# Two transformer blocks on one core: small first loads with matmuls on a constant ahead of them, side banks for a third product, and the last product one token half after the other

## The chip, the cores and the metric

The kernel runs on one NeuronCore of a Trainium2 chip. A core has a matrix engine (TensorE, "PE" in the profile, with its weight loads as "PEld"), a vector engine (VectorE, "DVE"), a scalar engine (ScalarE, "ACT"), GpSimd ("POOL") and SyncE ("SP"), which here issues nearly all DMAs. Each engine works through its own instructions in order; semaphores tie them together. TensorE writes to PSUM, which has eight banks. The metric is the device time of one execution in microseconds; shown are three runs and one more execution taken with the hardware profiler.

## The reference

Input is `x`, 512 tokens of width 1024, in fp32. What is computed:

```
u  = rmsnorm(x) * norm_g
x += mixer1(u)          # 4 mLSTM heads of 256, and compressed/selected/windowed attention
x += ffn1(rmsnorm(x))   # gated: 2 x 2816 wide in, 2816 wide out, behind two norms folded into one factor
x += mixer2(rmsnorm(x)) # gated delta rule beside pooling
x += ffn2(rmsnorm(x))   # as ffn1
out = rmsnorm(x) * final_g
```

Each of the stages is modulated by vectors that an `ada` part computes from a conditioning input. The rmsnorm needs the sum of squares over all 1024 columns of a token before its factor (`rstd`) is known.

## The kernel before

The tokens lie along the free dimension: `x` is eight tiles of 128 channels x 512 tokens. A product is a `Group`: an output tile of 128 channels (or 256 to 512 columns "token-major") summed over `kts` tiles of 128 inputs, in an fp32 emulation of three matmuls, hi x hi, hi x lo and lo x hi, where hi is the value rounded to the matmul's fp32r and lo the rest. A group's weights come in pieces of at most 1024 columns. For each piece SP issues a DMA to `wr` (three buffers; `load`, L302), ScalarE casts it to `wh` and VectorE, or in the mixer every third time GpSimd, subtracts to get `wl` (`part`, L306). `run` (L323) walks over the plan, stays two pieces ahead with the splits and further ahead with the DMAs, and between the steps of a product calls `side_step`, which lets generators (the norm, gates, attention, mLSTM, `ada`) emit a little work of their own. A tile scheduler then fixes each engine's order. Products write to four PSUM banks of the pool `pg`, side work to the four of `pb` (`bank`).

At a norm, TensorE doesn't wait for `rstd`: the first products of a stage take `u = x * g` without the factor (`halves=True`: the token halves 0 to 255 and 256 to 511 go to two banks, each weight being used for both), and their evacuation `unorm` multiplies by `rbc`, the factor broadcast over the partitions. Meanwhile the generator `norm` runs: `colsum` into `nsum` (a matmul with `ones` over `nacc`, the sum of squares), `rstd`, a broadcast by matmul (`rb`, with its cast `rbc`), and then the eight normed inputs, `ht` and their hi and lo parts `hh` and `hl`. For FFN1 (`i == 0`) there are two norms in a row and so a second factor, `rr`.

At the start `setup` issues the loads: `cols` (all column constants), then `x` tile by tile with the pieces of the first weight `w_v0` between them (3, 3 and 2 of its 288-column k-tiles), `cst` (identity, masks), `posi`. `block1`'s `begin` then makes `uh` and `ul` (hi and lo of `u`) in the same order, on ScalarE and VectorE, in an order kept by hand, and behind it adds squares to `nacc`. The first product is `w_v0`, the next, `pe`, is `w_v1`, whose two pieces are taken together (`early`). The mLSTM's gates are side work: `lir`, `lfr` rows, a scan `mrow` on VectorE, and small products `gcol`, the last of them on `mrow`.

At the end, product 7 of FFN2's output (`ev_last`, L1466) runs with `halves`, both token halves alternating but for its last piece, which does half 0 and then half 1. Behind half 0's last matmul its residual `xr` and squares `sq7` are taken; `final_norm` (L1475) sums them on TensorE and takes the root on GpSimd; `final` (L1486) broadcasts the factor (`r1b`), multiplies (`fin`, 16 instructions of 128x256) and stores, in eight DMAs of 256 KB.

Of the kernel before, what the change touches and what calls it, by code (L numbers as in the profile page):

```python
# [9 lines left out]
F32 = mybir.dt.float32  # L10
# [8 lines left out]
P = 128  # L19
# [10 lines left out]
SOLVE_STEP = 4  # L30
SOLVE_DELAY = 7
NV = 2
NG = 3
# [124 lines left out]
class Group:  # L158


    def __init__(self, src, width, kts, xs, evac, token_major=False, pre=None, halves=False, mid=None, early=0):
        self.mid, self.early = mid, early
# [14 lines left out]
class Builder:  # L177
# [145 lines left out]
    def run(self, plan, ahead_dma=3, ahead_split=2):  # L323
# [5 lines left out]
        for g in plan:  # L329
# [6 lines left out]
            for k0, n in g.pieces:  # L336
# [41 lines left out]
                elif g.halves:  # L378
                    if k0 == 0:
                        ps = [self.pg.tile([P, 512], F32, tag="g", name="pg") for _ in range(2)]  # L380
                    if g.mid and k0 + n == g.kts:

                        for c, (e, f) in enumerate(((0, 256), (256, 512))):
                            for k in range(n):
                                xh, xl = g.xs()[k0 + k]
                                a, b = hi[:, k * wd:(k + 1) * wd], lo[:, k * wd:(k + 1) * wd]
                                self.mm(ps[c][:, :256], a, xh[:, e:f], False, False)
                                self.mm(ps[c][:, :256], a, xl[:, e:f], False, False)
                                self.mm(ps[c][:, :256], b, xh[:, e:f], False, k == n - 1)
                                if c and k == n // 2:  # L390
                                    g.mid()
                            g.evac(c, ps[c])
                        i += 1
                        continue
                    for k in range(n):
                        xh, xl = g.xs()[k0 + k]
                        kk = k0 + k
                        for w, x, first, last in ((hi, xh, kk == 0, False), (hi, xl, False, False),
                                                  (lo, xh, False, kk == g.kts - 1)):
                            for c, (e, f) in enumerate(((0, 256), (256, 512 if g.mid else 514))):  # L400
# [26 lines left out]
    def setup(self):  # L427
        nc = self.nc
        self.cst = self.const(max(e for _, e in self.coff.values()), "cst")
        self.cols = self.const(max(e for _, e in COLS.values()), "cols")  # L430
        self.posi = self.const(NT, "posi", I32)
        self.x = []
        nc.sync.dma_start(self.cols, self.A["cols"])
        for kt in range(KT):
            if kt % 3 == 0:
                self.load(kt // 3 + 1)
            s = self.slot("x")
            nc.sync.dma_start(s, self.A["xt"][:, kt])
# [5 lines left out]
        self.ones = self.const(P, "ones")  # L444
        nc.vector.memset(self.ones, 1.0)
        self.mhalf = self.const(32, "mhalf")
        nc.vector.memset(self.mhalf, -0.5)
# [67 lines left out]
    def norm(self, i):  # L515
# [12 lines left out]
        if i == 0:  # L528
# [6 lines left out]
            r1, r = r, rr  # L535
        self.rcol = r
        if i is None:
# [213 lines left out]
    def block1(self):  # L751
# [135 lines left out]
        for h in range(4):  # L887
            if h == 0:
                plan.append(self.start_norm(None))
                us = lambda: self.u  # L890
                G(W["w_v0"][0], 288, KT, us, ev_v(0), True)
                for i in range(1, NV):
# [496 lines left out]
    def ffn(self, j, i):  # L1389
# [47 lines left out]
        for f in range(NH):  # L1437
            for up in range(2):
                w = W[f"f{j}i"][f + up * NH]
                if f < 3:  # L1440
                    plan.append(Group(w, P, KT, lambda: self.u, ev_u(f, up), halves=True))
                else:
# [14 lines left out]
        for f in range(KT):  # L1457
            if i == 2 and f == KT - 1:
                plan.append(Group(W[f"f{j}o"][f], P, NH, lambda: self.act_, self.ev_last, halves=True,
                                  mid=lambda: self.final_norm(0)))  # L1460
            else:
# [4 lines left out]
    def ev_last(self, c, ps):  # L1466
# [6 lines left out]
        self.act(self.sq7[:, h], s[:, h], AF.Square)  # L1473

    def final_norm(self, c):  # L1475

        b = self.bank("n4")
        for t in range(2):
            s = slice((2 * c + t) * P, (2 * c + t + 1) * P)
            self.mm(b[:, t:t + 1], self.nacc[:, s], self.ones[:, 0:1], True, False)  # L1480
            self.mm(b[:, t:t + 1], self.sq7[:, s], self.ones[:, 0:1], False, True)
        v, self.nr[c] = self.small(2, "nv"), self.small(2, "nr")
        self.ts(v, b[:, 0:2], 1.0 / D, EPS, OP.mult, OP.add)
        self.pow(self.nr[c], v, 2)

    def final(self):  # L1486
        def bcast(c):
            b = self.bank("r1b")
            for t in range(2):
                self.mm(b[:, t * P:(t + 1) * P], self.nr[c][:, t:t + 1].to_broadcast([P, P]), self.ident)  # L1490
            return b

        b = bcast(0)
        self.final_norm(1)
        for c in range(2):
            for f in range(0, KT, 2):
                s = self.slot("fin").rearrange("p (f t) -> p f t", f=2)
                for e in range(2):
                    self.stt(s[:, e], self.x[f + e][:, c * 256:c * 256 + 256], self.c("final_g2", f + e, f + e + 1),
                             b[:, 0:256], OP.mult, OP.mult)  # L1500
                (self.nc.sync if f % 4 else self.nc.scalar).dma_start(
                    self.out[:, f:f + 2, c * 256:c * 256 + 256], s)
            if c == 0:
                b = bcast(1)

    def mixer(self):
# [485 lines left out]
```

## Time and profile before

| | us |
|---|---|
| three runs | 1960.74, 1965.48, 1965.86 |
| median | 1965.48 |
| profiled execution | 1959.12 |
| its span (first to last instruction) | 1957.3 |
| TensorE busy | 1909.8 |
| VectorE, ScalarE, GpSimd busy | 1157.4, 782.4, 293.5 |

The mean granted clock of TensorE over the span is 0.992 of full speed. A timeline's row gives the start, the duration of what it holds (one instruction, or several of the same kind in a row), and in brackets how long the engine stood idle before it and which instruction's end released it. Matmuls are pipelined: the duration of one is longer than the distance to the next, so pitches are taken between starts.

### The profile page before, as it was taken

To read this page: it belongs to the slowest core of one execution; us is meant where nothing else is said; L and a number is where in the kernel's file an instruction comes from. 1 tells how busy PE (TensorE), PEld (TensorE's weight loads), DVE (VectorE), ACT (ScalarE), POOL (GpSimd) and SP (SyncE) were. 2 spreads that over 40 slices of the span, in tenths; PEclk is the share of its full clock that TensorE was granted. 3 is DMA by queue.
4 is the path that set the end of the run, shared out by engine and by line. 5 is a ranking of instruction groups with operands and counts; after the bars stand their busy time and mean duration, and the time that the engine had idled before them with its cause. 6 is when DMAs were issued, how large, how long until landed. Compare 5 with 4: busy or idle time off the path is not lost. (4 is left out here: it accounts for less than half of the span.)

```text
span 1957.3 us, 26994 instructions
## 1 busy us (share of the span) xinstructions
PE 1909.8 (98%) x10296; PEld 1579.1 (81%) x10296; DVE 1157.4 (59%) x2307; ACT 782.4 (40%) x1568; POOL 293.5 (15%) x232
## 2 busy tenths in 40 slices
PE   8999999999999999999999998999999999999998
PEld 7889988887677888878888887777778898888887
DVE  7876554446446797774335677969645574333322
ACT  6444443434444432223224555564443342222221
POOL 2000000003220540000004232234020160000000
PEclk9999999999999999999999999999899999999999
DMA  5632224221103348883333233331232323333332
GB/s 198 202 101 87 76 76 151 78 87 57 52 28 116 116 139 260 263 263 112 106 116 95 80 89 100 93 88 55 72 124 86 126 90 97 97 97 93 91 90 72
DMA packets 89746, 216.17 MB, mean 110 GB/s; under 512 B 23569, under 2 KB 34705, under 8 KB 89617
## 3 DMA queue, kind: packets, MB, share of 16 engines
q1 hardware_dynamic: 84864, 208.27, 34.6%
q10 hardware_dynamic: 4752, 6.18, 1.0%
q8 instruction: 81, 1.33, 0.3%
q14 instruction: 49, 0.39, 0.1%
HBM read 206.55 MB, written 7.34 MB: 109 GB/s over the span
## 5 line engine op out<-in xcount | busy, mean ns | idle before, releaser
L217 ACT ACTIVATE wh<-wr 128x1024 fp32r<-128x1024 f32 (+4 forms) x311 | 315.1, 1014 | 626.7 <-PE pg L229 314.9
L220 DVE TENSOR_TENSOR wl<-wr,wh 128x1024 fp32r<-128x1024 f32 (+4 forms) x289 | 341.1, 1180 | 352.5 <-ACT wh L217 349.9
L229 PE MATMUL pg<-hh,wh 128*128 128x512 f32 x1240 | 500.5, 404 | 1.3 <-DVE un L220 1.3
L229 PE MATMUL pg<-hl,wh 128*128 128x512 f32 x1240 | 492.1, 397 | 0.0
L229 PE MATMUL pg<-hh,wl 128*128 128x512 f32 x1240 | 491.8, 397 | 0.3 <-DVE wl L220 0.3
L229 PEld LDWEIGHTS pg<-hh,wl 128*128 128x128 f32 x1240 | 234.0, 189 | 55.6 <-DVE wl L220 1.1
L229 PEld LDWEIGHTS pg<-hh,wh 128*128 128x128 f32 x1240 | 234.5, 189 | 52.1 <-issue 1.9
L229 PEld LDWEIGHTS pg<-hl,wh 128*128 128x128 f32 x1240 | 234.5, 189 | 50.3 <-issue 0.7
L229 PE MATMUL pg<-wh,hh 128*128 128x256 f32 (+2 forms) x512 | 157.8, 309 | 0.5 <-ACT hh L217 0.4
L229 PE MATMUL pg<-wh,hl 128*128 128x256 f32 (+2 forms) x512 | 151.4, 298 | 1.0 <-DVE hl L220 0.9
L229 PE MATMUL pg<-wl,hh 128*128 128x256 f32 (+2 forms) x512 | 151.5, 296 | 0.0
L229 PE MATMUL pg<-fah,wl 128*128 128x512 f32 (+1 forms) x374 | 140.0, 381 | 0.0
L229 PE MATMUL pg<-fah,wh 128*128 128x512 f32 (+1 forms) x374 | 139.9, 381 | 0.0
L229 PE MATMUL pg<-fal,wh 128*128 128x512 f32 (+1 forms) x374 | 139.8, 381 | 0.0
L220 POOL TENSOR_TENSOR nacc<-nacc,sq 128x512 f32<-128x512 f32 x34 | 47.6, 1405 | 611.0 <-ACT sq L217 610.9
L226 DVE SCALAR_TENSOR_TENSOR adaw<-adaw,sc 128x512 f32<-128x512 f32 x144 | 94.2, 687 | 37.1 <-DMA adaw<-in_ada 36.8
L226 DVE SCALAR_TENSOR_TENSOR ca<-cx,cols,ca 128x511 f32<-128x511 f32 (+2 forms) x120 | 99.3, 827 | 25.8 <-ACT ca L217 23.9
L229 PEld LDWEIGHTS pg<-wh,hh 128*128 128x128 f32 x512 | 96.7, 189 | 8.2 <-issue 3.7
L229 PEld LDWEIGHTS pg<-wl,hh 128*128 128x128 f32 x512 | 96.6, 189 | 4.3 <-issue 1.0
L229 PEld LDWEIGHTS pg<-wh,hl 128*128 128x128 f32 x512 | 95.9, 188 | 5.1 <-DVE hl L220 2.1
L229 PEld LDWEIGHTS pg<-fah,wh 128*128 128x128 f32 x374 | 69.3, 188 | 14.6
L229 PEld LDWEIGHTS pg<-fal,wh 128*128 128x128 f32 x374 | 69.2, 188 | 14.7
(429 smaller groups left out, 3065.9 us busy)
## 6 DMA issues: line engine op xcount, KB each, us to landing
adaw<-in_ada SPq DMA_DIRECT2D x72, 512.0 KB
wr<-in_f1i SPq DMA_DIRECT2D x44, 512.0 KB
wr<-in_f2i SPq DMA_DIRECT2D x44, 512.0 KB
wr<-in_m_qkv SPq DMA_DIRECT2D x24, 512.0 KB
wr<-in_w_o SPq DMA_DIRECT2D x16, 512.0 KB
wr<-in_f1o SPq DMA_DIRECT2D x16, 512.0 KB
wr<-in_m_g SPq DMA_DIRECT2D x16, 512.0 KB
wr<-in_f2o SPq DMA_DIRECT2D x16, 512.0 KB
```

What stands on the lines that cost most here:

```text
L217: return self.nc.scalar.activation(out, in_, f, bias=bias, scale=scale, **k)
L220: return (eng or self.nc.vector).tensor_tensor(out, a, b, op)
L226: return self.nc.vector.scalar_tensor_tensor(out, a, s, b, op0=op0, op1=op1, **k)
L229: return self.nc.tensor.matmul(out, lhsT, rhs, start=start, stop=stop, **k)
```

## The change

1. The start. `w_v0` comes in four pieces of 1, 2, 3 and 2 k-tiles (`FIRST`). A small tile `ng` with the columns of `norm_g` is loaded first; `cols` follows behind `x`. Nine matmuls of 128x128 on the constant `ones` stand first on TensorE. One piece more in block 1's list moves the split-ahead by one piece.
2. The norms. For FFN1 the norm generator takes one more step before `rb`. The third product on unnormed input (FFN's `f == 1` gate, the mixer's third `m_g`) takes its banks from `pb` (`alt`); the norm gives its own banks up sooner.
3. The last product does token half 0 over all its 22 k-tiles, and then half 1. At steps of half 1 the hook `final_mid` puts in half 0's sums, its root, its `r1b`, its eight `fin` and its four stores, and the sums over `nacc` for half 1.

```diff
+FIRST = [0, 1, 3, 6]
+WARM = 9
...
-        self.pieces = [(k, min(n, kts - k)) for k in range(0, kts, n)]
+        self.pieces = split or [(k, min(n, kts - k)) for k in range(0, kts, n)]
...
                 elif g.halves:
                     if k0 == 0:
-                        ps = [self.pg.tile([P, 512], F32, tag="g", name="pg") for _ in range(2)]
-                    if g.mid and k0 + n == g.kts:
...
+                        pool, tag = (self.pb, "b") if g.alt else (self.pg, "g")
+                        ps = [pool.tile([P, 512], F32, tag=tag, name="pg") for _ in range(2)]
+                    if g.mid:
+
+                        if k0 == 0:
+                            whole = []
+                        whole += [(hi, lo, k) for k in range(n)]
+                        if k0 + n == g.kts:
+                            for c, (e, f) in enumerate(((0, 256), (256, 512))):
+                                for kk, (hi, lo, k) in enumerate(whole):
...
+                                    if c:
+                                        g.mid(kk)
+                                g.evac(c, ps[c])
+                            whole = None
...
-        nc.sync.dma_start(self.cols, self.A["cols"])
+        self.ones = self.const(P, "ones")
+        nc.vector.memset(self.ones, 1.0)
+
+        b = self.bank("warm")
+        for _ in range(WARM):
+            self.mm(b[:, 0:P], self.ones, self.ones)
+        b = None
+        self.ng = self.const(KT, "ng")
+        nc.sync.dma_start(self.ng, self.A["cols"][:, COLS["norm_g"][0]:COLS["norm_g"][1]])
         for kt in range(KT):
-            if kt % 3 == 0:
-                self.load(kt // 3 + 1)
             s = self.slot("x")
             nc.sync.dma_start(s, self.A["xt"][:, kt])
             self.x.append(s)
-        self.load(3)
+            if kt in FIRST:
+                self.load(FIRST.index(kt) + 1)
+        nc.sync.dma_start(self.cols, self.A["cols"])
+        self.load(4)
...
+        if i == 0:
+            yield
         bc = self.rows_to_bcast(r, "rb")
         self.rbc = self.slot("rbc")
         self.act(self.rbc, bc)
+        bc = None
...
                 for kt in range(KT):
-                    if kt % 3 == 0:
-                        self.part(kt // 3 + 1)
-                    self.u_add(kt, self.x[kt], self.c("norm_g", kt, kt + 1))
+                    if kt in FIRST:
+                        self.part(FIRST.index(kt) + 1)
+                    self.u_add(kt, self.x[kt], self.ng[:, kt:kt + 1])
...
+                    plan.append(Group(w, P, KT, lambda: self.u, ev_u(f, up), halves=True,
+                                      alt=f == 1 and not up))
...
+    def final_mid(self, kk):
+
+        if kk == 4:
+            self.final_sum(0)
+            self.final_norm(0)
+        elif kk == 9:
+            self.final_out(0)
+        elif kk == NH - 3:
+            self.final_sum(1)
...
     def final(self):
...
         self.final_norm(1)
...
+        self.final_out(1)
...
-            G(W["m_g"][f], P, KT, us, ev_gu(("p", f)), halves=True)
+            G(W["m_g"][f], P, KT, us, ev_gu(("p", f)), halves=True, alt=f == 2)
```

The scheduler's orders show more than the diff. First ScalarE at the start. `uh` are the hi parts of the eight `u`, `gtr` is the first reader of `cst`, `wh` of 128x1024 is the first piece of `w_v1`. Before, from the sixth `uh` on:

```order
L217 ACTIVATE uh_153<-x_109,cols_92 128x512
L217 ACTIVATE wh_157<-wr_111 128x576
L217 ACTIVATE uh_161<-x_113,cols_92 128x512
L217 ACTIVATE uh_165<-x_115,cols_92 128x512
L217 ACTIVATE gtr_176<-cst_91 128x128
L217 ACTIVATE nacc_179<-x_97 128x512
L217 ACTIVATE sq_181<-x_99 128x512
```

Of the change, from the sixth `uh` on:

```order
L220 ACTIVATE uh_171<-x_124,ng_106 128x512
L220 ACTIVATE wh_175<-wr_128 128x576
L220 ACTIVATE uh_179<-x_126,ng_106 128x512
L220 ACTIVATE wh_282<-wr_220 128x1024
L220 ACTIVATE uh_183<-x_130,ng_106 128x512
L220 ACTIVATE gtr_194<-cst_91 128x128
L220 ACTIVATE nacc_197<-x_108 128x512
L220 ACTIVATE sq_199<-x_112 128x512
```

The cast of `w_v1`'s first piece now stands ahead of the last `uh`; before it stood behind the squares, further down than shown. VectorE's subtraction of the same piece moves with it, to a place ahead of the last `ul`.

Second TensorE at the mLSTM's gates, where the last `gcol` reads `mrow`, a scan on VectorE. Before, it stands 30 matmuls behind the `gcol` on `ones`, within the third product on normed input:

```order
L229 MATMUL pg_730<-hl_525,wh_563 128x512
L229 MATMUL pg_730<-hh_524,wl_564 128x512
L229 MATMUL gcol_677<-cst_91,mrow_650 128x4 x4
L229 MATMUL pg_730<-hh_528,wh_563 128x512
L229 MATMUL pg_730<-hl_529,wh_563 128x512
```

Of the change, 11 matmuls behind it, still within the second product:

```order
L232 MATMUL pg_682<-hh_519,wl_413 128x512
L232 MATMUL pg_682<-hh_550,wh_412 128x512
L232 MATMUL pg_682<-hl_551,wh_412 128x512
L232 MATMUL gcol_695<-cst_91,mrow_668 128x4 x4
L232 MATMUL pg_682<-hh_550,wl_413 128x512
L232 MATMUL pg_748<-hh_312,wh_581 128x512
```

So 19 matmuls that came ahead of it now follow it, while `mrow` has the same number in VectorE's order in both.

Third TensorE in FFN1's norm, where `rb` broadcasts the second factor `rr`. Before:

```order
L229 MATMUL pg_6714<-uh_6574,wl_6586 128x258
L229 MATMUL rb_6739<-cst_91,rr_6705 128x128 x4
L229 MATMUL pg_6713<-uh_6620,wh_6585 128x256
L229 MATMUL pg_6714<-uh_6620,wh_6585 128x258
L229 MATMUL pg_6713<-ul_6621,wh_6585 128x256
L229 MATMUL pg_6714<-ul_6621,wh_6585 128x258
L229 MATMUL pg_6713<-uh_6620,wl_6586 128x256
L229 MATMUL pg_6714<-uh_6620,wl_6586 128x258
L229 MATMUL pg_6809<-uh_6299,wh_6629 128x256
```

Of the change:

```order
L232 MATMUL pg_6732<-uh_6592,wl_6604 128x258
L232 MATMUL pg_6731<-uh_6638,wh_6603 128x256
L232 MATMUL pg_6732<-uh_6638,wh_6603 128x258
L232 MATMUL pg_6731<-ul_6639,wh_6603 128x256
L232 MATMUL pg_6732<-ul_6639,wh_6603 128x258
L232 MATMUL pg_6731<-uh_6638,wl_6604 128x256
L232 MATMUL pg_6732<-uh_6638,wl_6604 128x258
L232 MATMUL rb_6781<-cst_91,rr_6723 128x128 x4
L232 MATMUL pg_6815<-uh_6317,wh_6647 128x256
```

The six matmuls on the last k-tile of the second product stand ahead of `rb` now. The third product's banks are those of the side pool.

## Rows read from the trace of the kernel before

**Rows 1.** The page: busy us, share of the span, instructions.

```profile
PE 1909.8 (98%) x10296; PEld 1579.1 (81%) x10296; DVE 1157.4 (59%) x2307; ACT 782.4 (40%) x1568; POOL 293.5 (15%) x232
```

**Rows 2.** TensorE's waits: releaser, us in total, times, longest.

```profile
PE pg L229 <- DVE un L220: 3.0, 4, 1.3
```

**Rows 3.** TensorE's timeline, start: start, duration, shapes [idle before <-releaser].

```profile
7.66 0.61 PE L229 MATMUL pg<-wh,uh 128*128 128x288 f32 x1 [7.66 <-ACT uh L217]
...
11.73 0.39 PE L229 MATMUL pg<-wl,uh 128*128 128x288 f32 x1
...
12.62 0.29 PE L229 MATMUL pg<-wl,uh 128*128 128x288 f32 x1
12.75 0.29 PE L229 MATMUL pg<-wh,ul 128*128 128x288 f32 x1
...
22.27 1.05 PE L229 MATMUL nsum<-ones,nacc 128*128 128x1 f32 x8 [0.20 <-DVE nacc L220]
...
25.62 0.56 PE L229 MATMUL pe<-wh,uh 128*128 128x256 f32 x1
...
28.97 0.29 PE L229 MATMUL pe<-wh,uh 128*128 128x256 f32 x1
```

**Rows 4.** VectorE's timeline at the start.

```profile
13.79 1.41 DVE L226 SCALAR_TENSOR_TENSOR ul<-x,cols,uh 128x512 fp32r<-128x512 f32 x2
...
15.81 4.67 DVE L220 TENSOR_TENSOR nacc<-nacc,sq 128x512 f32<-128x512 f32 x6
20.40 1.22 DVE L220 TENSOR_TENSOR wl<-wr,wh 128x1024 fp32r<-128x1024 f32 x1
21.53 0.68 DVE L220 TENSOR_TENSOR nacc<-nacc,sq 128x512 f32<-128x512 f32 x1
```

**Rows 5.** ScalarE's timeline at the start: first reader of `cst`.

```profile
14.42 0.31 ACT L217 ACTIVATE gtr<-cst 128x128 fp32r<-128x128 f32 x1 [0.33 <-DMA cst<-in_cst]
```

**Rows 6.** Bytes moved from 0 to 13.3 us, and from 0 to 14.6.

```profile
DMA packets 1916, 3.89 MB, mean 292 GB/s; under 512 B 256, under 2 KB 384, under 8 KB 1916
...
DMA packets 2153, 4.42 MB, mean 303 GB/s; under 512 B 360, under 2 KB 488, under 8 KB 2153
```

**Rows 7.** Table by stretch: us, busy by engine, granted clock, DMA.

```profile
26.00:27.00 1.00, 1.00 (x6) 1.00 (x6) 0.30 (x1) 1.00 (x4) 0.32 (x1) 0.50 0.69 283
```

**Rows 8.** TensorE around the gates' products.

```profile
50.80 0.48 PE L229 MATMUL pg<-hh,wh 128*128 128x512 f32 x1
...
57.60 0.40 PE L229 MATMUL pg<-hh,wl 128*128 128x512 f32 x1
59.20 1.05 PE L229 MATMUL gcol<-cst,mrow 4*128 4x4 f32 x8 [1.20 <-DVE mrow L1280]
```

**Rows 9.** VectorE around the gates.

```profile
44.59 0.17 DVE L226 SCALAR_TENSOR_TENSOR lf<-f,fa 128x16 f32<-128x16 f32 x1
...
57.93 1.21 DVE L1280 TENSOR_TENSOR_SCAN mrow<-lfr,lir 4x512 f32<-4x512 f32 x1
```

**Rows 10.** TensorE's gaps in FFN1's norm.

```profile
677.76 1.16 PE L229 MATMUL rb<-cst,rr 128*128 128x128 f32 x8 [1.76 <-DVE rr L220]
...
692.55 0.75 PE L229 MATMUL pg<-uh,wh 128*128 128x256 f32 x2 [0.77 <-DVE un L220]
...
699.37 0.75 PE L229 MATMUL pg<-uh,wh 128*128 128x256 f32 x2 [0.55 <-DVE un L220]
```

**Rows 11.** VectorE in FFN1's norm: the last `hl`.

```profile
709.94 0.68 DVE L220 TENSOR_TENSOR hl<-hf,hh 128x512 fp32r<-128x512 f32 x1
```

**Rows 12.** TensorE in the mixer's norm.

```profile
1068.32 0.39 PE L229 MATMUL pg<-wh,hh 128*128 128x264 f32 x1 [0.45 <-ACT hh L217]
```

**Rows 13.** The tail on VectorE, then the second `r1b` on TensorE.

```profile
1946.55 0.48 DVE L226 SCALAR_TENSOR_TENSOR xr<-pg,G,xr 128x256 f32<-128x256 f32 x1 [0.66 <-PE pg L229]
...
1948.48 5.56 DVE L226 SCALAR_TENSOR_TENSOR fin<-xr,cols,r1b 128x256 f32<-128x256 f32 x14
...
1949.39 0.71 PE L229 MATMUL r1b<-cst,nr 128*128 128x128 f32 x4 [1.03 <-POOL nr L248]
```

More of the change, by code (lines that the diff above doesn't have):

```diff
@@ L158, with __init__ @@
 class Group:
-    def __init__(self, src, width, kts, xs, evac, token_major=False, pre=None, halves=False, mid=None, early=0):
-        self.mid, self.early = mid, early
+    def __init__(self, src, width, kts, xs, evac, token_major=False, pre=None, halves=False, mid=None, early=0, alt=False,
+                 split=None):
+        self.mid, self.early, self.alt = mid, early, alt
         self.src, self.width, self.kts, self.xs, self.evac = src, width, kts, xs, evac
@@ L379, in run @@
                     if k0 == 0:
-                        ps = [self.pg.tile([P, 512], F32, tag="g", name="pg") for _ in range(2)]
-                    if g.mid and k0 + n == g.kts:
[L383 to L392, printed above, removed]
+                        pool, tag = (self.pb, "b") if g.alt else (self.pg, "g")
[7 more added lines that the diff above has]
+                                for kk, (hi, lo, k) in enumerate(whole):
+                                    xh, xl = g.xs()[kk]
+                                    a, b = hi[:, k * wd:(k + 1) * wd], lo[:, k * wd:(k + 1) * wd]
+                                    self.mm(ps[c][:, :256], a, xh[:, e:f], kk == 0, False)
+                                    self.mm(ps[c][:, :256], a, xl[:, e:f], False, False)
+                                    self.mm(ps[c][:, :256], b, xh[:, e:f], False, kk == g.kts - 1)
+                                    if c:
+                                        g.mid(kk)
+                                g.evac(c, ps[c])
+                            whole = None
                         i += 1
@@ L399, in run @@
                                                   (lo, xh, False, kk == g.kts - 1)):
-                            for c, (e, f) in enumerate(((0, 256), (256, 512 if g.mid else 514))):
+                            for c, (e, f) in enumerate(((0, 256), (256, 514))):
                                 self.mm(ps[c][:, :f - e], w[:, k * wd:(k + 1) * wd], x[:, e:f], first, last)
@@ L536, in norm @@
         self.rcol = r
+        b = None
         if i is None:
@@ L890, in block1 @@
                 us = lambda: self.u
-                G(W["w_v0"][0], 288, KT, us, ev_v(0), True)
+                G(W["w_v0"][0], 288, KT, us, ev_v(0), True,
+                  split=[(k, n - k) for k, n in zip(FIRST, FIRST[1:] + [KT])])
                 for i in range(1, NV):
@@ L1473, in ev_last, with final_sum, final_norm @@
         self.act(self.sq7[:, h], s[:, h], AF.Square)
-    def final_norm(self, c):
-        b = self.bank("n4")
+    def final_mid(self, kk):
[6 more added lines that the diff above has]
+            self.final_sum(1)
+    def final_sum(self, c):
+        b = self.nb = self.bank("n4")
         for t in range(2):
             s = slice((2 * c + t) * P, (2 * c + t + 1) * P)
-            self.mm(b[:, t:t + 1], self.nacc[:, s], self.ones[:, 0:1], True, False)
-            self.mm(b[:, t:t + 1], self.sq7[:, s], self.ones[:, 0:1], False, True)
+            self.mm(b[:, t:t + 1], self.nacc[:, s], self.ones[:, 0:1], t == 0, False)
+    def final_norm(self, c):
+        b, self.nb = self.nb, None
+        for t in range(2):
+            s = slice((2 * c + t) * P, (2 * c + t + 1) * P)
+            self.mm(b[:, t:t + 1], self.sq7[:, s], self.ones[:, 0:1], False, t == 1)
         v, self.nr[c] = self.small(2, "nv"), self.small(2, "nr")
@@ L1484, in final_norm, with final_out @@
         self.pow(self.nr[c], v, 2)
-    def final(self):
[L1487 to L1493, printed above, removed]
-        self.final_norm(1)
[L1495 to L1504, printed above, removed]
+    def final_out(self, c):
+        b = self.bank("r1b")
+        for t in range(2):
+            self.mm(b[:, t * P:(t + 1) * P], self.nr[c][:, t:t + 1].to_broadcast([P, P]), self.ident)
+        for f in range(0, KT, 2):
+            s = self.slot("fin").rearrange("p (f t) -> p f t", f=2)
+            for e in range(2):
+                self.stt(s[:, e], self.x[f + e][:, c * 256:c * 256 + 256], self.c("final_g2", f + e, f + e + 1),
+                         b[:, 0:256], OP.mult, OP.mult)
+            (self.nc.sync if f % 4 else self.nc.scalar).dma_start(
+                self.out[:, f:f + 2, c * 256:c * 256 + 256], s)
+    def final(self):
+        self.final_norm(1)
+        self.final_out(1)
     def mixer(self):
```

5 lines of the change are left out of this document (1 added, 4 removed).

## The prediction

> **What bounds the kernel now.** I read the page's busy shares first: TensorE is busy for 98% of the span [rows 1]. So no engine's total matters here, only the gaps of TensorE and what ends each of them. The list of its waits names them by releaser, among them 3.0 us in four waits on an evacuation `un` [rows 2]. Then I read the timeline of TensorE where the change puts its hands, and beside it the engine that ends the gap.
>
> The start: the first product begins at 7.66 us and runs at a pitch of 0.24 us until 11.73; from there it is 0.13 (12.62 to 12.75) [rows 3]. Yet this product isn't what the next stage waits for. `nsum`, at 22.27, waits for VectorE's last addition to `nacc` (21.53 + 0.68) [rows 3, 4]; `rb` and the second product `pe` (25.62) hang on it. The chain of the start is therefore DMA, ScalarE, VectorE's row of `ul`, casts, `nacc`, and only then TensorE.
>
> Duration of the kernel: the profiled execution took 1959.12 us, the lower edge of the three runs. I make the sum against it and add it to their median, 1965.48, since the comparison will be of medians. What a measurement here can't tell from no change is 0.3%, 5.9 us.
>
> **The change part by part.**
>
> *Start.* Small pieces, the little `ng` and the warm matmuls let the first product begin sooner, and its 17 slow steps (7.66 to 11.73) could run at the quick pitch: 17 x (0.24 - 0.13), some 1.8 us. That time is won in front of the wait for `nacc`, so it lands in that wait unless VectorE is sooner too. VectorE is not: the planner hands out one piece more before the norm, and the order of ScalarE now has the cast of the first `w_v1` piece, a 128x1024 `wh`, between the seventh and eighth `uh`, and that of VectorE its `wl` between the seventh and eighth `ul`; before, they stood behind the squares. ScalarE can't pass it, so the eighth `uh`, the squares and `nacc` wait for that piece's DMA. When does it land? Before, the transfers through `cst` are 3.89 MB, a total reached at 13.3 us, and the first reader of `cst` started at 14.42 [rows 5, 6]: 1.1 us behind the bytes. The `w_v1` piece is 0.52 MB more, and 4.42 MB were reached at 14.6 [rows 6]; SP's queue has it behind `cst` and `posi` still. So it lands at about 15.7. From there: `wh` 1.0 (16.7), `wl` 1.2 (17.9), the last `ul` 0.7 (18.6), casts 0.6 (19.2), six `nacc` 4.67 (23.9), a `wl` 1.2 and the last `nacc` 0.7: 25.7 against 22.2 [rows 4]. **+3.5 us.** Ends: +4.7 if the bytes come 1.2 later behind the finer loads, -1.8 if the piece has landed before VectorE gets there and the quicker first product passes through whole. I take the middle of the working, since the 15.7 is read from two byte totals. The low clock of the first `pe` matmuls (0.50 in the row of 26 to 27 us [rows 7], until 28.97) stays in either case: TensorE idles ahead of it now as then.
>
> *Gates of the mLSTM.* TensorE's order has one more difference: the small `gcol` products on `mrow` stand 11 `pg` matmuls behind the first `gcol`, where there were 30. 19 matmuls at (57.60 - 50.80)/29 = 0.234 us [rows 8] are 4.5 us by which TensorE arrives sooner. `mrow` itself is a scan on VectorE that starts 13.3 us after `lf` (44.59, 57.93) [rows 9], and it stays at the same number in VectorE's row, behind the ada products. One `wl` (1.2) less stands ahead of it, but ScalarE has now two table loads between the two `scth` that feed that row, some 2 us more: between -1.1 and +0.8 for `mrow`. Before, TensorE waited 1.20 at this place [rows 8]; now 4.6 to 6.5, and since it does nothing meanwhile and all of block 1 is queued behind, I count **+4.2** (from +3.3 to +5.3). A gap of this size also costs clock: after the norm's gaps at 22 to 25.6 us the granted clock was 0.50 (1.2 GHz of 2.4) from 25.62 to 28.97 [rows 3, 7], so half of 3.3 us was lost: **+1.5** (0 if the clock holds). I take it whole, as the rows of the start are the nearest.
>
> The Trainium skill, page "TensorE: Matmul & The Clock Gate", section "Why this matters for your kernels", warns of idle gaps between bursts of matmuls, behind which the clock is throttled again. The rows at 25.62 and 28.97 agree. By that rule the 1.5 stands; if it didn't hold here, the sum would be 5.6.
>
> *FFN1's norm.* One more `yield` moves the six last matmuls of the second product ahead of `rb`, into the 1.76 us that TensorE waited for `rr` [rows 10]. The third product takes side banks, so it starts without the evacuation of the first, and the waits on `un` of 0.77 and 0.55 [rows 10] go: together up to 3.5 us earlier at the end of the sixth product. Next late is VectorE: the products on normed input need all eight `hl`, the last of which started at 709.94 before [rows 11], and its row behind `rb` has the same work in a different order, with a `fal` and an `adaw` ahead of the last `hl`, so about 711 now. TensorE, sooner, waits some 2 us for it. **-1.5** (from -3.5, if the `hl` are sooner as well, to -0.3).
>
> *Mixer's norm.* TensorE's order is the same; one `wl` less stands between GpSimd's `hf`, which can take away the waits of 0.4 on `hh` and `hl` [rows 12]: **-0.6** (-0.9 to +0.5). Through the added piece every third `wl` that goes to GpSimd is another one in the rest of the mixer (21 of them instead of 22): 0, and 2.5 to either side, as 1.2 us for one `wl` on VectorE is about what a chain there can gain or lose twice.
>
> *FFN2's norm.* TensorE's and VectorE's orders are equal there, and so are the releasers: 0.
>
> *Tail.* Half 0's eight `fin` and its four stores now run below the last product's second half. Behind the last product there remain `xr`, the sums, `nr`, `r1b` and eight `fin`. From `xr` (1946.55) to the second `r1b` there were 2.84 us, 0.71 for it, then 8 x 0.397 = 3.18 (5.56/14): 6.7, where the last `fin` ended 7.5 behind that `xr` (1948.48 + 5.56) [rows 13]. That is 0.8 less. But the sum over `nacc` for half 1 and `r1b` for half 0 (0.71) now stand between the last product's matmuls and so ahead of `xr`: 0.8 more. **0** (-0.8 to +0.6). The drain behind the last `fin` is as before.
>
> Sum: 3.5 + 4.2 + 1.5 - 1.5 - 0.6 = **+7.1 us**: 1966.2 against the profiled 1959.12, and 1965.5 + 7.1 = **1972.6** against the median, +0.36%.
>
> **The rivals.**
>
> *A. It does what it says.* The `w_v1` piece lands before the eighth `uh`, or doesn't gate it. For it: x and all pieces are asked for sooner. Against it: SP's queue, where the piece stands behind `cst` and `posi`. Then the start is -1.8, FFN1 gets its -3.5 and the mixer -0.9, with 4.2 still lost at `gcol`: -2.0, 1963.5, not slower. It decides from a landing before 13 us. If `gcol` costs nothing in addition (because `mrow`'s row too is through sooner), it is -6.2, 1959.3, faster.
>
> The Trainium skill has a rule for this side, in the same section of the page "TensorE: Matmul & The Clock Gate": matmuls ahead of those that count, so that these run at the full clock. By it alone the start would be 1.8 shorter and the time 1963.7. The trace of before agrees on the slow pitch, but shows that `nacc` is waited for.
>
> *B. The waits are covered.* The start costs +1, since the piece lands at 13.2 or so, and the wait at `gcol` grows by 3.3 without loss of clock; FFN1 and mixer as in my sum: 1.0 + 3.3 - 2.1 = +2.2, 1967.7, within the bound. For it: each is the low end of a term here. Against it: three low ends at once.
>
> *C. It adds up.* Start +4.7, `gcol` +5.3 and +1.5, FFN1 only -0.3, the mixer's other split +2.5: +13.7, 1979.2. For it: all on one chain of TensorE. Against it: four high ends.
>
> **How the numbers follow.** My forecast (slower, around +7) has 0.42; its own range is 1968 to 1977. B 0.30, A 0.20 (a quarter of it faster beyond the bound, the rest within), C 0.08. Faster by over 0.3%: 0.05 of A, and I add 0.07 because the mixer's unread terms and the spread of the runs (5 us) could carry a case of A or B beyond -5.9: 0.12. Slower by over 0.3%: 0.42 + 0.08 = 0.50, less 0.04 of forecasts that end just inside: 0.46. Within: 0.42. Eight in ten lie between B and A on one side and most of C on the other: 1960 to 1978.
>
> **What would show it.** Right: the first product starts near 5.7, but `nsum` only at 25 to 26 with a gap of over 4 us ahead of it, released by VectorE; the eighth `uh` directly behind a `wh` that waited for a DMA; a wait on `mrow` of 4 to 6.5 us at a granted clock that falls behind it; no waits on `un` in FFN1's third and fifth product, and one of about 2 us on the last `hl`. Wrong: `nsum` before 22 us (the start), a wait on `mrow` below 3 us (the gates), FFN1's products on normed input over 2.5 us nearer to their norm's start. The forecast as a whole falls if the start and the gates together cost less than 4 us.

## The result and the profile after

The changed kernel takes 1982.64 us in the median (four runs, 1979.50 to 1983.46) against 1963.11 us of the kernel before in the same session: a ratio of 1.0102, 95% interval 1.0079 to 1.0126. That is +19.5 us where +7.1 was forecast, and 4.6 us beyond the upper end of the range. The sign was right, the size was not. The profiled execution took 1981.95 us, its span is 1980.2.

The page's first part, in the columns of [rows 1]:

```profile
PE 1921.7 (97%) x10314; PEld 1589.7 (80%) x10314; DVE 1165.1 (59%) x2309; ACT 784.9 (40%) x1570; POOL 290.5 (15%) x231
```

TensorE is busy for 11.9 us more than in [rows 1], with 18 instructions more (the nine warm products are two each): these products are 4.2 us of it, and matmuls at half clock are busy for longer. The other 11 of the 22.9 us between the two spans are idle. TensorE's timeline of the changed kernel, as in [rows 3], to the first product of the gates:

```profile
1.04 4.21 PE L232 MATMUL warm<-ones 128*128 128x128 f32 x18 [1.04 <-DVE ones L443]
5.68 0.40 PE L232 MATMUL pg<-wh,uh 128*128 128x288 f32 x1 [0.43 <-ACT uh L220]
...
27.02 1.87 PE L232 MATMUL nsum<-ones,nacc 128*128 128x1 f32 x8 [4.09 <-DVE nacc L223]
30.23 2.08 PE L232 MATMUL rb<-cst,r 128*128 128x128 f32 x8 [1.35 <-POOL r L251]
31.96 0.56 PE L232 MATMUL pe<-wh,uh 128*128 128x256 f32 x1
...
36.16 0.32 PE L232 MATMUL pe<-wl,uh 128*128 128x256 f32 x1
...
38.60 0.35 PE L232 MATMUL pe<-wh,uh 128*128 128x256 f32 x1 [1.66 <-DVE gng L229]
...
52.85 0.38 PE L232 MATMUL lir<-cst,li 128*4 128x128 f32 x2
```

The first product does begin 2 us sooner (5.68 for 7.66), and at the quick pitch: 0.13 us, where before it was 0.24 until 11.73. But `nsum` waits 4.09 us for `nacc` and comes at 27.02 instead of 22.27. `rb`, at 30.23, takes 2.08 us where it took 1.29 before, `pe` starts 6.3 us later than before, at the slow pitch until 36.16, and stops once more for 1.66 us on an evacuation, `gng`. When the gates' first product `lir` starts, at 52.85, 8.7 us are lost (44.17 before). ScalarE shows why `nsum` is late, as [rows 5]:

```profile
17.12 1.06 ACT L220 ACTIVATE wh<-wr 128x1024 fp32r<-128x1024 f32 x1 [2.15 <-DMA wr<-in_w_v]
18.09 0.71 ACT L220 ACTIVATE uh<-x,ng 128x512 fp32r<-128x512 f32 x1
```

The cast of `w_v1`'s first piece stands ahead of the eighth `uh` and waits 2.15 us for its DMA, which landed at 17.1. SP's timeline has that piece's issue:

```profile
11.54 1.70 SPq L305 DMA_DIRECT2D wr<-in_w_v  x2
```

Before, it was issued 1.6 us sooner:

```profile
9.91 1.66 SPq L302 DMA_DIRECT2D wr<-in_w_v  x2
```

And VectorE's shows the reason of the second stop:

```profile
35.09 1.00 DVE L229 SCALAR_TENSOR_TENSOR hl<-ht,cols,hh 128x512 fp32r<-128x512 f32 x1 [6.00 <-ACT hh L220]
...
38.23 0.23 DVE L229 SCALAR_TENSOR_TENSOR gng<-pg,r,cols 128x24 f32<-128x24 f32 x1
```

It stood idle 6.00 us for the first `hh`, with two `hl` ahead of the evacuations (`mv`, `gif`, `gng`) that free the first product's banks for `pe`. Before, those evacuations stood ahead of the first `hl`:

```profile
27.18 0.48 DVE L226 SCALAR_TENSOR_TENSOR mv<-pg,r,mv 128x256 fp32r<-128x256 f32 x1 [0.88 <-ACT mv L217]
...
28.76 1.01 DVE L226 SCALAR_TENSOR_TENSOR hl<-ht,cols,hh 128x512 fp32r<-128x512 f32 x1
```

The gates, as in [rows 9] on VectorE and [rows 8] on TensorE:

```profile
50.65 0.17 DVE L229 SCALAR_TENSOR_TENSOR lf<-f,fa 128x16 f32<-128x16 f32 x1
...
63.82 1.21 DVE L1301 TENSOR_TENSOR_SCAN mrow<-lfr,lir 4x512 f32<-4x512 f32 x1
```

```profile
65.08 1.05 PE L232 MATMUL gcol<-cst,mrow 4*128 4x4 f32 x8 [3.27 <-DVE mrow L1301]
```

The wait is 3.27 for 1.20. In the table by stretch (columns as in [rows 7], the granted clock third from the right) the clock is at half, 1.2 GHz, at 32 us, behind `gcol` and in FFN1's norm:

```profile
32.00:34.00 2.00, 2.00 (x11) 2.00 (x11) 0.00 (x0) 0.60 (x1) 0.98 (x1) 0.50 0.17 66
...
68.00:70.00 2.00, 2.00 (x6) 1.55 (x5) 2.00 (x9) 0.00 (x0) 0.00 (x0) 0.50 0.85 188
726.00:728.00 2.00, 1.85 (x5) 1.29 (x5) 2.00 (x5) 0.70 (x1) 0.00 (x0) 0.50 0.18 12
```

TensorE in FFN1's norm, as in [rows 10]:

```profile
691.34 1.16 PE L232 MATMUL rb<-cst,rr 128*128 128x128 f32 x8 [1.05 <-DVE rr L223]
...
717.06 0.47 PE L232 MATMUL pg<-hh,wh 128*128 128x512 f32 x1 [0.72 <-DVE un L223]
...
724.65 0.50 PE L232 MATMUL pg<-hh,wh 128*128 128x512 f32 x1 [2.00 <-ACT hh L220]
```

The waits of 0.77 and 0.55 on `un` are gone. Among the products on normed input a new one of 0.72 on `un` has come, and one of 2.00 on the last `hh`, with a half clock behind it. The mixer's waits by releaser, of the changed kernel from 1080 to 1480 us:

```profile
PE dgq L232 <- ACT dkd L220: 5.2, 3, 2.7
PE ppw L232 <- DVE pll L229: 2.1, 1, 2.1
...
PE dks L232 <- DVE dws L1964: 1.8, 1, 1.8
...
PE dgp L232 <- DVE dg L229: 1.4, 1, 1.4
```

and of the kernel before in the same window:

```profile
PE dks L229 <- DVE dws L1931: 0.8, 1, 0.8
...
PE dgq L229 <- ACT dkd L217: 0.5, 1, 0.5
...
PE dgp L229 <- DVE dg L226: 0.3, 1, 0.3
```

The products `dgq` waited 0.5 us before and wait 5.2 now; `ppw` isn't in the list of before at all. The tail on TensorE and VectorE, as in [rows 13]:

```profile
1969.21 0.28 PE L232 MATMUL pg<-fah,wl 128*128 128x256 f32 x1
1970.52 0.61 PE L232 MATMUL n<-ones,sq 128*128 128x1 f32 x4 [1.02 <-ACT sq L220]
1972.15 1.22 PE L232 MATMUL r1b<-cst,nr 128*128 128x128 f32 x4 [1.03 <-POOL nr L251]
```

```profile
1969.53 0.48 DVE L229 SCALAR_TENSOR_TENSOR xr<-pg,G,xr 128x256 f32<-128x256 f32 x1 [1.49 <-PE pg L232]
...
1973.41 3.22 DVE L229 SCALAR_TENSOR_TENSOR fin<-xr,cols,r1b 128x256 f32<-128x256 f32 x8 [2.09 <-PE r1b L232]
```

Eight `fin` remain where there were sixteen behind the last product. From the last matmul of the last product to the end of the span it is 10.99 us (1969.21 to 1980.2), and was 11.07 (1946.23 to 1957.3); the last `r1b` took 1.22 where it took 0.71.

### The profile page after: what moved, and what is told of

Read it like the earlier page. It is cut to its first block, busy times and chain, and to the rows that moved or that the text cites. A ratio compares the mean times of both kernels' runs of the same rounds, so it can differ in the third digit from the quotient of the medians.

```text
span 1980.2 us, 27041 instructions
## 1 busy us (share of the span) xinstructions
PE 1921.7 (97%) x10314; PEld 1589.7 (80%) x10314; DVE 1165.1 (59%) x2309; ACT 784.9 (40%) x1570; POOL 290.5 (15%) x231
## 5 line engine op out<-in xcount | busy, mean ns | idle before, releaser
L232 PEld LDWEIGHTS pg<-fah,wh 128*128 128x128 f32 x374 | 70.2, 188 | 14.6
```

Source lines behind the costliest of these rows:

```text
L232: return self.nc.tensor.matmul(out, lhsT, rhs, start=start, stop=stop, **k)
```

## The experiments

The kernel before ran beside every one of them, so each has its own ratio. To see where a kernel falls behind, I took the start of the same product from the timelines of TensorE and subtracted that of the first profile of before:

| profile | `lir` | `mR`, first | `nsum`, FFN1 | second `rb`, FFN1 | `nsum`, mixer | `dgp`, mixer | `nsum`, FFN2 | span |
|---|---|---|---|---|---|---|---|---|
| before, start in us | 44.17 | 67.33 | 670.40 | 705.45 | 1047.10 | 1081.03 | 1578.44 | 1957.3 |
| before_again | +1.8 | +3.0 | +6.1 | +6.1 | +5.4 | +5.4 | +5.6 | +5.6 |
| start_036 | 0.0 | +1.7 | +4.6 | +4.6 | +3.8 | +3.8 | -0.8 | -0.7 |
| norm_only | -0.6 | +1.1 | +4.6 | +1.0 | +4.4 | +4.4 | +2.5 | +1.9 |
| start_025 | +5.7 | +7.5 | +7.1 | +7.1 | +6.4 | +6.6 | +1.7 | +1.9 |
| start_pool | +8.6 | +13.1 | +15.0 | +15.1 | +13.7 | +13.9 | +8.8 | +9.2 |
| start_only | +9.4 | +11.3 | +13.0 | +13.0 | +11.9 | +13.3 | +16.5 | +17.0 |
| start_0245 | +6.8 | +10.2 | +12.3 | +13.5 | +12.1 | +13.6 | +20.2 | +20.6 |
| the change | +8.7 | +11.9 | +13.6 | +9.8 | +13.8 | +15.2 | +21.5 | +22.9 |

**Each part alone.** The first four separate the parts. start_only undoes parts 2 and 3 of the change (of part 3 the fence shows only the hook; the loop of the last product and `final` go back with it):

```diff
-        b = None
...
-        if i == 0:
-            yield
...
-        bc = None
...
-                    plan.append(Group(w, P, KT, lambda: self.u, ev_u(f, up), halves=True,
-                                      alt=f == 1 and not up))
+                    plan.append(Group(w, P, KT, lambda: self.u, ev_u(f, up), halves=True))
...
-                                  mid=self.final_mid))
+                                  mid=lambda: self.final_norm(0)))
...
-            G(W["m_g"][f], P, KT, us, ev_gu(("p", f)), halves=True, alt=f == 2)
+            G(W["m_g"][f], P, KT, us, ev_gu(("p", f)), halves=True)
```

> The kernel before with part 1 of the change alone (four pieces of w_v0, ng first, cols behind x, nine matmuls on a constant). Theory O (orders): the fourth piece moves the order of all engines, in the gates and in the mixer too, and nearly all of the loss is here: +18 to +22 us against before, pe at 31 to 32 us, the wait on mrow above 3 us. Rival N (the norm's side banks and the tail carry half of it): +8 to +12.

Measured: 1977.26 against 1963.20, ratio 1.0078 (1.0062 to 1.0093): +14 us in the medians, +15 by the ratio (12 to 18). That is less than theory O said, whose low end the interval just reaches, and more than N. `pe` starts at 31.20, as O said, but the wait on `mrow` is 1.97, not above 3. Three quarters of the loss are in part 1.

norm_only keeps part 2 alone; against before:

```diff
+        b = None
...
+        if i == 0:
+            yield
...
+        bc = None
...
-                    plan.append(Group(w, P, KT, lambda: self.u, ev_u(f, up), halves=True))
+                    plan.append(Group(w, P, KT, lambda: self.u, ev_u(f, up), halves=True,
+                                      alt=f == 1 and not up))
...
-            G(W["m_g"][f], P, KT, us, ev_gu(("p", f)), halves=True)
+            G(W["m_g"][f], P, KT, us, ev_gu(("p", f)), halves=True, alt=f == 2)
```

> The kernel before with part 2 alone (one step more in FFN1's norm, side banks for a third product). Theory O: FFN1's waits on un go, a wait on the last hh or hl comes, and nothing outside the norms changes: between -3 and +3 us. Rival N: +6 or more, most of it behind the mixer's norm.

Measured: 1962.09, ratio 1.0003 (0.9990 to 1.0016): no change, as O said. The table shows that it is no zero inside: 3.6 us are won up to FFN1's second `rb` and 3.4 are gone again at the mixer's norm.

tail_only keeps part 3 alone, with the last product's loop, `final_mid` and `final` of the change; against before:

```diff
-                                  mid=lambda: self.final_norm(0)))
+                                  mid=self.final_mid))
...
```

> The kernel before with part 3 alone (last product one token half after the other). Theory O: the products between the last matmuls cost what the shorter row of fin gains: 0 to +1 us, with the last fin 0.8 us nearer to the last matmul. Rival: it gains what it was meant for, 2 us or more, since half of the stores are gone before the end.

Measured: 1963.34, ratio 1.0006 (0.9992 to 1.0020): +0.1 us in the median, as the forecast had it. In its profile the last `fin` ends 6.91 us behind the start of the last matmul of the last product, 7.81 before: 0.9 nearer, as theory O said. The rival's 2 us lie just outside the interval.

start_036 is start_only with the pieces of before:

```diff
-FIRST = [0, 1, 3, 6]
+FIRST = [0, 3, 6]
-        self.load(4)
+        self.load(len(FIRST))
```

> The kernel before with ng first, cols behind x and the nine matmuls on a constant, but w_v0 in the three pieces of before (3, 3, 2 k-tiles). The cast of w_v1's first piece then stands behind the squares again, and the gates and the mixer have the orders of before. Theory O: the whole loss is gone, -2 to +1 us against before. Rival L (the loads themselves are at fault: cols and cst later, SP's queue longer): +5 or more, with nsum behind 25 us.

Measured: 1962.07, ratio 1.0000 (0.9989 to 1.0012). `ng` first, `cols` behind `x` and the warm matmuls together change the time by no more than 2.4 us either way, and `nsum` is at 22.52: the rival L falls. All of the loss of start_only hangs on the list of `w_v0`'s pieces. What a quick first product is worth isn't tested by this kernel: in its profile the first product starts at 7.25, 0.4 us sooner than before, and runs at the slow pitch until 13.12.

**What the fourth piece does.** It changes three things at once: the place of the early cast, the order behind it (evacuations, gates), and the count by which `wl` go to GpSimd. Other cuts take them apart, since the orders that come out of the scheduler differ. start_025 has three pieces and yet the early cast:

```diff
-FIRST = [0, 1, 3, 6]
+FIRST = [0, 2, 5]
```

> The kernel before with the new loads and the matmuls on a constant, but w_v0 in three pieces of 2, 3 and 3 k-tiles: the cast of w_v1's first piece stands ahead of the eighth uh, as in the change; the evacuations, the gates and GpSimd's share in the mixer are as before. Theory O: this cast alone holds nsum back to about 27 us and lengthens the low clock behind it: +5 to +7 us. Rival P (the fourth piece is all of it, through the orders behind the start): -1 to +1.

Measured: 1966.55 against 1963.01, ratio 1.0012 (0.9999 to 1.0026), +3.5 us in the medians and +2.4 by the ratio; its TensorE shows

```profile
26.44 1.87 PE L232 MATMUL nsum<-ones,nacc 128*128 128x1 f32 x8 [2.86 <-DVE nacc L223]
...
65.14 1.05 PE L232 MATMUL gcol<-cst,mrow 4*128 4x4 f32 x8 [1.30 <-DVE mrow L1292]
```

so `nsum` is 4.2 us late, nearly as in the change, and `gcol` waits 1.30, as before. At `lir` the profile is 5.7 behind that of before, but before_again, the same kernel as before, is 1.8 behind as well: some 4 us are the cast's, in the profile, and the runs say between 0 and 5. Theory O's +5 to +7 is missed at the low end; the rival P is not excluded by the runs, though `nsum`'s place is against it.

start_0245 has four pieces, with the early cast behind the squares:

```diff
-FIRST = [0, 1, 3, 6]
+FIRST = [0, 2, 4, 5]
```

> As start_only, but with four pieces of 2, 2, 1 and 3 k-tiles, by which the cast of w_v1's first piece stands behind the squares; the first hl stand ahead of the first product's evacuations, and gates and mixer have the change's orders. Theory O: nsum at 22 to 23 us, but a wait of pe on an evacuation, the longer wait on mrow and the mixer's share stay: +7 to +10. Rival E (the early cast is all of it): -1 to +1.

Measured: 1977.40, ratio 1.0069 (1.0054 to 1.0083), +13.5 us by the ratio: more than O said, and E falls. Its TensorE:

```profile
23.55 1.05 PE L232 MATMUL nsum<-ones,nacc 128*128 128x1 f32 x8 [1.55 <-DVE nacc L223]
...
35.24 0.55 PE L232 MATMUL pe<-wh,uh 128*128 128x256 f32 x1 [2.18 <-DVE gng L229]
```

`nsum` is only 1.3 us later than before, and the wait on the evacuation is there nevertheless (2.18). So the early cast, on which my working of the start rested, is not needed for most of the loss.

start_pool is start_only with one number changed:

```diff
-eng=nc.gpsimd if self.poolpart and i % self.poolpart == 0 else None)
+eng=nc.gpsimd if self.poolpart and (i - 1) % self.poolpart == 0 else None)
```

> As start_only, but the count by which every third wl goes to GpSimd is put back by one, so that the mixer has the split and nearly the order of before; the start and the gates are as in the change. Theory O: the mixer's part of the loss goes, 4 to 6 us of the 14 to 15: +8 to +11. Rival: the mixer's part comes from something else, +13 to +16.

Measured: 1972.64, ratio 1.0045 (1.0030 to 1.0059), +9 us, against +14 to +15 for start_only: as O said, some 5 us (4.4 by the medians, 6.5 by the ratios) are the mixer's and hang on which third of the `wl` GpSimd takes. Its mixer waits from 1080 to 1480 us:

```profile
PE doT L235 <- DVE dot L229: 7.7, 4, 3.3
PE dqt L235 <- ACT dvr L220: 3.4, 2, 2.2
PE diq L232 <- DMA dtm<-tdr: 1.7, 1, 1.7
...
PE dks L232 <- DVE dws L1943: 0.8, 1, 0.8
```

No wait of `dgq` or `ppw` of that size is left. In the table start_pool comes 5.1 us nearer between `dgp` and FFN2's `nsum`, where start_only, start_0245 and the change fall back by 3 to 7 more; but start_036, which has the mixer of before, comes 4.6 nearer too, and before_again doesn't. The busy time of TensorE tells the two effects apart. In that stretch it is idle for 18.0 us before, 17.4 in start_036 and 17.2 in start_pool, and for 22.8, 24.8 and 22.3 in start_only, start_0245 and the change: 4 to 7 us of waits come with the other split. Its busy time for the same products is 479.5 us before, 475.4 in start_036, 475.2 in start_pool and 481.3 in the change, which goes with the clock: it is at half for 20.5, 10.2, 10.2 and 23.9 us there. In the changed kernel the instruction `dkd`, on which `dgq` waits, stands on ScalarE behind a `ct`:

```profile
1132.93 0.63 ACT L220 ACTIVATE ct<-ca 128x512 f32<-128x512 f32 x1 [6.62 <-DVE ca L229]
1133.47 1.12 ACT L220 ACTIVATE dkd<-dkt,dkd 128x128 f32<-128x128 f32 x4
```

which had waited 6.62 us for VectorE's `ca`; start_pool's waits 3.23 there.

**The base.** before_again is the kernel before, unedited, with a second profile.

> The kernel before, unchanged, profiled once more. Theory C (whether the clock falls behind a wait of 1.2 to 1.5 us differs from one execution to the next): its waits are those of the first profile, but a stretch of low clock stands behind the wait on mrow at 59 us or on cw at 309 us, and the span is 2 to 5 us longer than 1957.3. Rival: the same stretches at the same places, span within 1 us.

Measured: 1964.75 us, span 1962.9, 5.6 more than the first. Its waits on `mrow` (1.18) and on `cw` (1.77) are about those of the first profile (1.20 and 1.54), but the stretch table reads

```profile
62.00:64.00 2.00, 2.00 (x7) 1.56 (x6) 1.97 (x9) 1.34 (x3) 0.00 (x0) 0.54 0.68 233
316.00:318.00 2.00, 2.00 (x9) 1.88 (x9) 0.27 (x2) 0.32 (x1) 0.00 (x0) 0.50 0.34 116
```

where the first profile has

```profile
62.00:64.00 2.00, 2.00 (x10) 1.60 (x9) 2.00 (x5) 0.70 (x1) 0.00 (x0) 1.00 0.67 238
316.00:318.00 2.00, 2.00 (x11) 1.65 (x11) 0.25 (x1) 1.50 (x3) 0.00 (x0) 1.00 0.96 365
```

The span is 0.6 us beyond what theory C said, and its rival falls. norm_only, tail_only and start_036 have the same two half-clock stretches. Of all profiles here, 13 of 14 have half the clock behind the wait on `mrow`, and behind the wait on `cw` ten of the twelve in which the first block has it. So the clock falls behind these waits in most executions, and didn't in the one that I predicted from.

**All parts with the pieces of before.** after_036:

```diff
-FIRST = [0, 1, 3, 6]
+FIRST = [0, 3, 6]
```

> The changed kernel, all three parts, with one number other: w_v0 in the three pieces of before (3, 3, 2 k-tiles), so that the orders of start, gates and mixer are those of before. Theory O (the piece count, not what the parts mean to do, makes the loss): -1 to +3 us against before, against +20 of the change. Rival S (the side banks and the tail cost some 5 us on top whenever they stand together): +5 or more.

Measured: 1964.84 against 1962.36, ratio 1.0012 (0.9997 to 1.0026). One list of numbers takes away 17 of the 19.5 us; S's +5 is the interval's upper end.

**Two attempts to keep a gain.** norm_ny3456 is norm_only with FFN1's `hh` and `hl` emitted closer together:

```diff
             self.h.append((hi, lo))
-            yield
+            if not (i == 0 and kt in (3, 4, 5, 6)):
+                yield
```

> Part 2 alone, and in FFN1's norm four of the eight steps that make hh and hl are emitted together, so that ScalarE's last hh stand ahead of the tanh and the cast of the third product pair. Theory H (what the side banks gain in front of the products on normed input is given back to the last hh, which is queued behind these two): the wait of 2.0 us on hh goes and 2 to 3.5 us of gain stay, -2 to -4 against before. Rival: VectorE's hl or GpSimd's hf is as late, within 1 us of before.

Measured: 1967.01, ratio 1.0028 (1.0011 to 1.0045), slower. Theory H falls: the wait on `hh` is gone, but

```profile
713.53 0.76 PE L232 MATMUL pg<-hh,wh 128*128 128x512 f32 x1 [5.30 <-DVE un L223]
```

now a bank's evacuation is 5.30 us late. On VectorE it stands behind five `hl`, the first at 706.29, and VectorE doesn't idle between them:

```profile
712.98 0.74 DVE L223 TENSOR_TENSOR un<-pg,rbc 128x256 f32<-128x256 f32 x2
```

In norm_only the same evacuation, at 707.61, has three of the `hl` behind it. With the sooner `hh` more `hl` stand ahead of the evacuation, and the wait went from `hh` to a bank.

cps_late moves the compression's products by one side step:

```diff
             yield
             yield
+            yield
             ps = self.bank("cps")
```

> The kernel before, with the compression's products cps one side step (12 matmuls) later, so that their weights' DMA has landed. Theory C (the clock falls behind that wait in most executions): the wait of 1.5 us goes and the low clock of some 6 us behind it too: -2 to -4.5 us. Rival W (the small cps products themselves bring the clock down): only the wait goes, -1.5 us or less, and the low stretch is still there.

Measured: 1965.28, ratio 1.0018 (1.0001 to 1.0036). Neither theory's time. The first block ran without a wait, at a granted clock of 1.00, but the second, whose weights are issued right ahead of it, got the wait instead:

```profile
344.44 1.27 PE L229 MATMUL cps<-kk,cw 128*128 128x66 f32 x8 [1.63 <-DMA cw<-in_c_w]
```

and the half clock lies behind that one, from 346 to 354 us. cps_later gives both blocks four steps between the issue of their weights and their products, where before has two and cps_late three (the expectation below says three, but the edit makes four):

```diff
             yield
-            yield
+            for _ in range(1 + 3 - 1):
+                yield
             ps = self.bank("cps")
```

> The kernel before, with both blocks of the compression's products cps put three side steps behind the issue of their weights instead of two. Theory C (the clock falls behind the wait on cw): neither block waits for cw, the clock stays at 1.00 in both places, and the kernel is 2 to 5 us faster than before. Rival M (the wait moves again, to kk or to the next consumer, and the low clock with it): between -1 and +3 us.

Measured: 1959.34 against 1962.45, ratio 0.9985 (0.9972 to 0.9997), 3 us faster than before and the fastest of all kernels here. Its two blocks and the clock there:

```profile
314.96 4.00 PE L229 MATMUL cps<-kk,cw 128*128 128x66 f32 x32
...
345.14 4.00 PE L229 MATMUL cps<-kk,cw 128*128 128x66 f32 x32
```

```profile
316.00:318.00 2.00, 2.00 (x19) 2.00 (x18) 0.00 (x0) 0.00 (x0) 0.00 (x0) 1.00 0.73 233
...
347.00:349.00 2.00, 2.00 (x19) 2.00 (x19) 0.71 (x1) 0.00 (x0) 0.00 (x0) 1.00 0.10 41
```

The same small products, without a wait ahead of them, leave the clock at 1.00, here twice and once in cps_late. That is theory C's outcome: in these three places `cps` by itself doesn't bring the fall. The time alone doesn't decide it, as the interval (-5.5 to -0.6 us) reaches into M's range.

## Why the prediction was wrong

*Start* (+3.5 forecast; +8.7 at `lir` in the profile: 4.8 up to `nsum`, 1.6 more up to `pe` and 2.3 within `pe`). The mechanism that the forecast names was there, with its signs: the eighth `uh` behind a `wh` that waits for its DMA, and a gap of 4.09 ahead of `nsum`. The term was mis-sized, and a second wait was missing. "So it lands at about 15.7" was taken from bytes alone; the piece was issued 1.6 us later than before, at 11.54, and landed at 17.1, which put `nsum` at 27.02 instead of the 25.7 worked out, at the term's own upper end. That the low clock "stays in either case" was wrong for this profile: `nsum` and `rb` ran at half clock as well, and `pe` until 36.16, 4.2 us where it had been 3.35. That the longer idle stretch did this isn't shown: in before_again `rb` took 2.08 us as well, behind the same wait as before (0.72), and in start_only `nsum` took 1.05 behind a wait of 3.73. And VectorE's row behind `r1v` wasn't read: its `hl` ahead of the evacuations cost TensorE 1.66 us, and 2.18 in start_0245, where the cast is on time. By the runs, the early cast that I held for the whole term is worth 0 to 5 us (start_025), which the 3.5 fits; but start_0245 loses 13.5 without it.

*Gates* (+4.2 and +1.5). The longer wait came, and smaller: 3.27 - 1.20 = +2.1. `mrow` kept its distance from `lf` (13.2 us, 50.65 to 63.82; 13.3 before) and TensorE did come 4.4 us sooner; but `lf`, for which `lfr` had waited, now started 2.4 us ahead of it (53.06) where it had been 0.2, so `mrow` had 2.2 us of a start that I didn't count. The 1.5 for the clock was a misreading: the kernel before has that half clock itself in most executions, as before_again shows at 62 us; of the 14 profiles here only the one that I predicted from lacks it. A loss that both have is none.

*FFN1* (-1.5). Up to the products on normed input it gained 3.8 (13.6 to 9.8 in the table), just beyond the far end of my range; the waits of 0.72 on a bank and 2.00 on the last `hh`, and the half clock at 726 us, go with its loss (13.8 at the mixer's norm). norm_only repeats the gain and the two waits (0.64 and 2.02) at the full clock, and is 0 by the runs. I had the 2 us and named the wrong tile (`hl`, which is behind this `hh`), and not the clock.

*Mixer* (-0.6 for its norm, 0 for the rest). This is the step that failed, by 8 us where the start's miss is 5: "0, and 2.5 to either side, as 1.2 us for one `wl` on VectorE is about what a chain there can gain or lose twice". The norm lost 1.4 instead (a wait of 1.36 on `dg` at `dgp`, 1.17 on `hl`), and behind it 6.3 us went: 4.4 of idle time, through the waits on `dkd` and `pll`, and 1.9 of busy time with the clock. By the runs of start_pool the split alone makes some 5 us. A moved piece is not worth its own 1.2 us, but what the chain behind it is late, and each new gap of TensorE can take its clock as well.

*FFN2 and tail* (0 and 0). FFN2 was 1.4 us off, with a half clock at 1634 us that the profile of before doesn't have. In the tail the sum was right: tail_only has the 0.8 that eight fewer `fin` were to gain (0.9) and is no faster, +0.1 in the median. That the products between the last product's matmuls took it back is below what the runs can tell. In the change only 0.4 of it is left (7.42 us from the last matmul to the last `fin`'s end), as its `r1b` ran at half clock.

*The rivals.* A fell with `nsum`. B's small wait at `gcol` came, even smaller, its small start didn't. C, "four high ends", came nearest, at +13.7, but not by its ends: the gates stayed below the forecast, and the start and the mixer went beyond C. The chance of 0.08 was too small since I treated the ends as independent: those of the start and the mixer hang on one cause, the fourth piece.

What stays open: by the medians the parts alone sum to +14 - 1 + 0 = +13 us, all together to +19.5; by the ratios they sum to 0.87%, 17 us, against 1.02% (interval +15 to +25). The runs show no difference between the sum and the whole. In the profiles the change falls back by 11.7 us between FFN1's second `rb` and FFN2's norm, start_only by 3.5. Of that difference 5.1 lie in FFN1, where the change gives back its gain, and 3.1 behind `dgp`, where both have the same orders: TensorE's idle time is 22.3 us for 22.8 there, its busy time 3.5 us more, so that this part goes with the clock. It was not tried to move VectorE's evacuations back with four pieces, by which the loss at the gates and that at `pe` could be told apart.

## What to carry to other kernels

A list of pieces that also serves as a count (who takes every third one, how far ahead a planner works) makes a change at the start a change of the whole kernel: compare the orders to the end, and expect a moved piece to cost what the chain behind it loses, not its own duration. The gain of an earlier start lands in the next wait, so ask first what the stage behind it waits for, and read every engine's row up to there. A single profile is one draw of the clock: before a term is taken from it, look whether a second profile of the same kernel has it too.

## What was not expected of the hardware

The same wait of 1.2 to 1.8 us was followed by the full clock in one execution of a kernel and by half of it in another: 1.00 at 62 and 316 us in the first profile, 0.54 and 0.50 in the second, 5.6 us of span apart with the same instructions in the same order. The Trainium skill, page "TensorE: Matmul & The Clock Gate", Part 1, says that how many matmuls run slowly at a start varies between runs of one kernel; the two profiles agree, with the slow pitch until 11.73 us in one and 10.69 in the other, and show the same for the fall behind a short wait. And the warm matmuls were no sure warm start: of the seven profiles that have them, the first product ran at the full clock throughout in two (the change and start_025), at half clock for a stretch in four, and in start_036, where it starts 2.00 us behind them, until 13.12. Nor does the length of a wait tell by itself what follows: start_025's `nsum` took 1.87 us, at half clock, after a wait of 2.86, and start_only's 1.05 after 3.73.
